# Scan state and its output as whole-array products on a block diagonal, with two state buffers, in a hybrid decoder layer

## The chip, the cores and the metric

The kernel runs on one core of one Trainium2 chip. The metric is the device time in microseconds (us) from launch to end; lower is better. The engines of the core are TensorE (matrix products; PE in the profile, its weight loads PEld), VectorE (DVE), ScalarE (ACT), GpSimd (POOL) and SyncE (SP, which issues DMAs).

## What is computed

One decoder layer over 16 meta tokens and 512 positions, model width 2048, all in fp32: a gated short convolution and an RWKV-7 recurrence side by side on one input projection, an output projection, then a gated feed-forward part. The change touches the recurrence alone. The reference, cut to that:

```python
def rwkv7_scan(r, w, k, v, a_vec, b_vec):
    """All inputs (B, L, H, N) float32. State S (B, H, N_v, N_k):
    S_t = S_{t-1} diag(w_t) + (S_{t-1} a_t) b_t^T + v_t k_t^T ; y_t = S_t r_t."""
    ...
    def step(s, inp):
        r_t, w_t, k_t, v_t, a_t, b_t = inp
        sa = jnp.einsum('bhvk,bhk->bhv', s, a_t)
        s = s * w_t[:, :, None, :] + sa[..., None] * b_t[:, :, None, :] + v_t[..., None] * k_t[:, :, None, :]
        y_t = jnp.einsum('bhvk,bhk->bhv', s, r_t)
        return s, y_t
    s0 = jnp.zeros((bsz, h, n, n), jnp.float32)
    _, ys = lax.scan(step, s0, xs)
    return jnp.swapaxes(ys, 0, 1)
```

There are 16 heads of size 64.

## The kernel before

The sequence of 528 positions is cut into 17 chunks of 32 (`NC`, `C`). Two heads make a pair `P` (128 partitions), two pairs make a scan `s`; so there are 4 scans of 17 chunks, one after the other, each with four heads: `p` is the pair in the scan and `h` the head in the pair. `prep` builds the operands of a pair (among them `XR`, the decayed queries and keys, and `PC`, the decay over a chunk), `inverse` solves the triangular systems within the chunks on VectorE and leaves them in `AT`, and `moves` puts the keys and b vectors into `BK` and the values into `VT`.

`scan(s)` (line 1020) does for each chunk `c`:

- GpSimd copies the chunk's values from `VT` into the state tile `cur` (lines 1029 to 1033). A state tile `SUV` is 128 partitions x 2 pairs x 2 heads x 64: for head `h` the 64 partitions from `64 * h` hold the state, and the other 64 hold the chunk's values and the solved vectors. There are three of them, taken in turn (lines 633 and 1026).
- One product `xp` of `XR` with the whole `cur` (line 1038), four ScalarE copies to `x0`, one product `up` with `AT` (line 1046), and four ScalarE copies of it into `cur`.
- The next state (lines 1059 to 1076): GpSimd multiplies the old state by the decay (`s0`), four products of 64x64 weights from `BK` with 64 columns of `cur` write `sp`, one for each pair and head, and VectorE adds `sp` and `s0` into the next state tile `nxt`.
- The output (lines 1077 to 1083): four products with `cur[:, p, h]` as weights (128 rows, 64 columns) and 32 columns of `XR` write `yp`, and ScalarE copies it to `yt`.

`xp`, `up`, `sp` and `yp` share two PSUM buffers (`st`). All products of the scan are plain fp32. Those of the projections run in the F32R type, on high and low parts of the operands.

The scans run inside the first phase of the kernel, whose other work on TensorE is the input projection (`rkv`, `conv`, written to `mps` and scaled there), LoRA products and block sums. Generators of all tasks are drawn in an order set by a clock of assumed costs (lines 1168 to 1240): the scan's steps have rank 2, the projections' products the rank `FILL`, which stands behind all others. What is drawn is not issued at once: the class `Plan` keeps every instruction with its dependences, and `order` (line 354) makes the order of all engines at once by list scheduling, with the durations of `time` (line 293), the tile shape of a product by `mode` (line 329) and costs for changing it (lines 481 to 484). The engines then run their queues in that order. A product of other than 128x128 weights counts 0.055 there, an fp32 product of the whole array at least 0.222. The scheduler also plans the first and last units of the feed-forward phase; its middle is written in a fixed order.

Since `Engine.__getattr__` issues everything, nearly all rows of the profile name line 231; the tiles tell them apart. In the rows, "st<-SUV,BK" are the state products, "st<-XR,SUV" with 128x64 weights the output products, "st<-SUV,XR" is `xp`, "st<-x,AT" is `up`.

## Time and profile before

| what | us |
|---|---|
| median of 3 runs | 2372.61 |
| the three runs | 2370.54 to 2372.68 |
| profiled execution | 2370.47 |
| its span, from the first to the last instruction | 2368.7 |
| TensorE busy | 2345.2 |
| VectorE busy | 1744.6 |
| ScalarE busy | 1225.2 |
| GpSimd busy | 636.1 |

The profile is of one execution. Its rows give a start or a busy time in us and the mean duration of one instruction in ns. Products are pipelined, so the record of one is longer than the time by which it moves the next; what a product costs is read from the starts of its neighbours. "x8" behind a product counts records, and an fp32 product leaves two (the weights are loaded in two parts).

### The profile page before, as it was taken

The page shows a single profiled execution, that of the slowest core. Times are in us where ns is not written, and L with a number is a line of the kernel's source. Part 1 is how long each engine was busy: PE and PEld are TensorE (multiplying, and loading weights), DVE is VectorE, ACT ScalarE, POOL GpSimd, SP SyncE. Part 2 cuts the span into 40 slices and gives each one's busy share as a digit, 9 for nine tenths or more (in the row PEclk, how much of TensorE's full clock was granted, in tenths as well). Part 3 has the DMA queues.
Part 4 walks back from the last instruction along what each step waited for, and adds up shares of the span by engine and source line. Part 5 has one row for each costly group of instructions (what it writes and reads, how often), then busy time and mean ns, then how long its engine had stood idle before and what let it go on. Part 6 is the DMA issues. An engine that isn't in the chain of part 4 may idle for free.

```text
span 2368.7 us, 46298 instructions
## 1 busy us (share of the span) xinstructions
PE 2345.2 (99%) x18450; PEld 2238.2 (94%) x18450; DVE 1744.6 (74%) x2366; ACT 1225.2 (52%) x2402; POOL 636.1 (27%) x755
## 2 busy tenths in 40 slices
PE   9999999999999999999999999999999999999997
PEld 8999999999999999998989899999999998989897
DVE  7687888878754677784868686777767686859585
ACT  7666766766654555574434343343434342525255
POOL 0232747465351011510202121211212120202025
PEclk9999999999999999999999999999999999999998
DMA  5444332333433755913333323242423242323344
GB/s 185 158 126 122 90 97 83 104 111 98 132 99 95 232 170 178 214 57 100 108 107 103 112 82 124 81 134 81 124 75 125 70 135 79 124 82 105 97 142 90
DMA packets 138759, 274.14 MB, mean 116 GB/s; under 512 B 31120, under 2 KB 54288, under 8 KB 138544
## 3 DMA queue, kind: packets, MB, share of 16 engines
q1 hardware_dynamic: 131760, 264.35, 36.2%
q0 software_dynamic: 6784, 6.83, 2.0%
q8 instruction: 145, 2.38, 0.4%
q14 instruction: 70, 0.57, 0.1%
HBM read 245.30 MB, written 25.84 MB: 114 GB/s over the span
## 4 chain that ended last, share of the span: by engine, by line
PE 96%; DVE 1%; DMA 1%; POOL 1%; ACT 1%; issue 0%; DVEq 0%; SPq 0%; ACTq 0%; POOLq 0%
PE mps L231 60%; PE u L231 18%; PE d L231 11%; PE st L231 4%; PE aux L231 3%; DMA acc<-xT_dram 1%; DVE acc L231 0%; POOL acc L231 0%; PE psn L231 0%; DVE q L231 0%; DMA l<-lo 0%; DMA raw<-w_in_dram 0%; ACT whi L231 0%; POOL XR L231 0%; ACT q L231 0%
## 5 line engine op out<-in xcount | busy, mean ns | idle before, releaser
L231 ACT CAST H<-R 128x1024 fp32r<-128x1024 f32 x401 | 420.4, 1049 | 474.9 <-PE u L231 180.7
L231 DVE TENSOR_TENSOR O<-R,H 128x1024 fp32r<-128x1024 f32 x401 | 521.7, 1301 | 124.2 <-ACT H L231 116.8
L231 PE MATMUL mps<-ahi,whi 128*128 128x264 f32 (+2 forms) x1792 | 360.0, 289 | 6.1 <-ACT ahi L231 5.5
L231 PE MATMUL mps<-alo,whi 128*128 128x264 f32 (+2 forms) x1792 | 360.2, 289 | 0.0
L231 PE MATMUL mps<-ahi,wlo 128*128 128x264 f32 (+2 forms) x1792 | 358.0, 288 | 1.2 <-DVE wlo L231 1.0
L231 PE MATMUL mps<-tt,H 128*128 128x258 f32 x2160 | 288.2, 283 | 1.0 <-ACT q L231 0.9
L231 PEld LDWEIGHTS mps<-ahi,whi 128*128 128x128 f32 x1792 | 273.8, 189 | 9.1 <-ACT ahi L231 5.8
L231 PEld LDWEIGHTS mps<-ahi,wlo 128*128 128x128 f32 x1792 | 274.0, 189 | 3.6 <-DVE wlo L231 1.6
L231 PEld LDWEIGHTS mps<-alo,whi 128*128 128x128 f32 x1792 | 274.0, 189 | 2.8 <-DVE alo L231 0.6
L231 DVE TENSOR_TENSOR wlo<-raw,whi 128x512 fp32r<-128x512 f32 x261 | 199.2, 768 | 104.8 <-ACT whi L231 88.0
L231 PEld LDWEIGHTS mps<-tt,H 128*128 128x128 f32 x2160 | 272.6, 189 | 2.4 <-ACT q L231 1.1
L231 POOL TENSOR_TENSOR raw<-raw,rb 128x516 f32<-128x516 f32 (+1 forms) x45 | 92.8, 2062 | 668.7 <-DVE raw L231 630.6
L231 PE MATMUL mps<-alo,H 128*128 128x258 f32 x1064 | 258.3, 284 | 0.4 <-DVE alo L231 0.4
L231 PE MATMUL mps<-ahi,H 128*128 128x258 f32 x1064 | 258.0, 282 | 0.0
L231 POOL TENSOR_TENSOR R<-R 128x1024 f32<-128x1024 f32 x40 | 131.5, 3287 | 419.1 <-DVE R L231 419.1
L231 ACT CAST whi<-raw 128x512 fp32r<-128x512 f32 x261 | 160.7, 619 | 137.5 <-PE mps L231 83.9
L231 DVE TENSOR_TENSOR R<-R 128x1024 f32<-128x1024 f32 x136 | 226.4, 1665 | 1.7 <-DMA R<-w_pair_dram 0.4
L231 PEld LDWEIGHTS mps<-alo,H 128*128 128x128 f32 x1064 | 198.4, 189 | 0.9 <-DVE alo L231 0.6
L231 PEld LDWEIGHTS mps<-ahi,H 128*128 128x128 f32 x1064 | 198.7, 190 | 0.0
L231 POOL TENSOR_SCALAR SUV<-VT 32x64 f32<-32x64 f32 x272 | 129.4, 476 | 161.4 <-PE st L231 137.5
L231 PE MATMUL mps<-ahi,O 128*128 128x258 f32 x1064 | 157.5, 283 | 0.0
L231 PE MATMUL mps<-tt,O 128*128 128x258 f32 x1080 | 153.4, 281 | 0.0
(339 smaller groups left out, 4593.5 us busy)
## 6 DMA issues: line engine op xcount, KB each, us to landing
R<-w_gu_dram SPq DMA_DIRECT2D x176, 512.0 KB, 3.5
raw<-w_in_dram SPq DMA_DIRECT2D x208, 256.0 KB, 2.7
R<-w_down_dram SPq DMA_DIRECT2D x88, 512.0 KB, 3.7
raw<-w_out_dram SPq DMA_DIRECT2D x32, 256.0 KB, 3.6
R<-w_pair_dram SPq DMA_DIRECT2D x16, 512.0 KB, 4.3
l<-lo SPq DMA_DIRECT2D x24, 264.0 KB, 2.1
R<-ysp SPq DMA_DIRECT2D x14, 257.0 KB, 4.3
lo<-l SPq DMA_DIRECT2D x12, 264.0 KB, 2.6
```

Of the source, the lines that this page charges most:

```text
L231: return getattr(self.real, op)(*real, **{k: x.get() if isinstance(x, View) else x for k, x in kw.items()})
```

## The change

The two heads of a pair are taken together in the state and output products. A new tile `BD` (128 x 2 pairs x 2 heads x 64), set to zero once, gets the chunk's two blocks of `BK` on its diagonal by two GpSimd copies. The state product of a pair then has 128x128 weights (`BD[:, p]`) and 128 columns (both heads of `cur[:, p]`); the blocks of `sp` off the diagonal aren't read. The output product of a pair has `cur[:, p]` of both heads as 128x128 weights and 64 columns of `XR`; of `yp`, too, only the diagonal blocks are read, by two ScalarE copies. There are two state tiles instead of three. In the planner, fp32 products lose their lower bound of 0.222, and a change of type from fp32 to F32R within the whole-array shape counts 0.085.

```diff
@@ -298,9 +298,9 @@
             n *= s
         psum = any(a.tile.pool.space == "psum" for a in x["ins"])
         if e == "PE":
-            if self.mode(x) != (128, 128):
+            if self.mode(x)[:2] != (128, 128):
                 return 0.055
-            return max(0.222, n / 600 + 0.004) if x["args"][1].tile.dtype is F32 else n / 2400 + 0.0115
+            return n / 600 + 0.012 if x["args"][1].tile.dtype is F32 else n / 2400 + 0.0115
         if e == "SP":
             return 0.42
         if e == "POOL":
@@ -329,7 +329,7 @@
     def mode(self, x):
 
         w = x["args"][1]
-        return tuple(next(i for i in (32, 64, 128) if i >= n) for n in (w.parts, int(np.prod(w.shape[1:]))))
+        return tuple(next(i for i in (32, 64, 128) if i >= n) for n in (w.parts, int(np.prod(w.shape[1:])))) + (w.tile.dtype,)
 
     def two(self, x):
 
@@ -440,7 +440,7 @@
         free, busy = dict.fromkeys(HOP, 0.0), dict.fromkeys(HOP, (0.0, False))
         free["PE"] = self.head
         ring = []
-        self.pipe, table, kind = 0.0, 0, (128, 128)
+        self.pipe, table, kind = 0.0, 0, (128, 128, F32R)
         began, ends = [0.0] * len(units), [0.0] * len(units)
         for u in range(len(units)):
             if not left[u]:
@@ -481,7 +481,11 @@
             if e == "PE":
                 k = self.mode(x)
                 if k != kind:
-                    d, kind = d + (0.25 if k == (128, 128) else 0.1), k
+                    if k[:2] != kind[:2]:
+                        d += 0.25 if k[:2] == (128, 128) else 0.1
+                    elif k[2] is F32R:
+                        d += 0.085
+                    kind = k
             began[u], ends[u] = t, start + d
             free[e], busy[e] = start + d, (start + d, self.two(x))
             dma = x["op"] == "dma_start"
@@ -630,10 +634,13 @@
         gmask = cst[:, :64]
         smask = cst[:, 64:]
         SUV = []
-        for i in range(3):
+        for i in range(2):
             t = p1.tile([128, 2, 2, 64], F32, name=f"SUV{i}")
             G.memset(t, 0.0)
             SUV.append(t)
+
+        BD = p1.tile([128, 2, 2, 64], F32, name="BD")
+        G.memset(BD, 0.0)
 
 
         AT = p1.tile([128, NC, 2, 2, C], F32, name="AT")
@@ -1023,7 +1030,7 @@
             f = F3 if s == NP // 2 - 1 else 1
             yt = p1.tile([128, 2, L], F32, name="yt", bufs=2)
             for c in range(NC):
-                cur, nxt = SUV[c % 3], SUV[(c + 1) % 3]
+                cur, nxt = SUV[c % 2], SUV[(c + 1) % 2]
                 b, c0 = (0, 0) if c < CH[1][0] else (1, CH[1][0])
                 BK, VT = st["f", s, b]
                 for h in range(2):
@@ -1057,30 +1064,34 @@
                 elif c > 8:
                     st["late", s] = True
                 if c < NC - 1:
-                    sp = stp.tile([128, 2, 64], F32, name="st")
+                    sp = stp.tile([128, 2, 2, 64], F32, name="st")
+                    for h in range(2):
+                        o = slice(64 - 64 * h, 128 - 64 * h)
+                        G.tensor_scalar(out=BD[o, :, h], in0=BK[o, :, c - c0], scalar1=1.0, scalar2=None, op0=ALU.mult)
+                    for p in range(2):
+                        PE.matmul(sp[:, p], BD[:, p].rearrange("r h k -> r (h k)"), cur[:, p].rearrange("r h v -> r (h v)"),
+                                  start=True, stop=True)
                     for h in range(2):
                         q = slice(64 * h, 64 * h + 64)
-                        o = slice(64 - 64 * h, 128 - 64 * h)
                         if c:
                             if not h:
                                 s0 = p1.tile([128, 2, 64], F32, name="s0")
                             G.tensor_tensor(out=s0[q], in0=cur[q, :, h],
                                             in1=PC[q, :, c - 1].unsqueeze(2).to_broadcast([64, 2, 64]), op=ALU.mult)
-                        for p in range(2):
-                            PE.matmul(sp[q, p], BK[o, p, c - c0], cur[o, p, h], start=True, stop=True)
                     for h in range(2):
                         q = slice(64 * h, 64 * h + 64)
                         if c:
-                            V.tensor_tensor(out=nxt[q, :, h], in0=sp[q], in1=s0[q], op=ALU.add)
+                            V.tensor_tensor(out=nxt[q, :, h], in0=sp[q, :, h], in1=s0[q], op=ALU.add)
                         else:
-                            V.tensor_copy(nxt[q, :, h], sp[q])
-                yp = stp.tile([128, 2, C], F32, name="st")
+                            V.tensor_copy(nxt[q, :, h], sp[q, :, h])
+                yp = stp.tile([128, 2, 2, C], F32, name="st")
                 for p in range(2):
-                    for h in range(2):
-                        q = slice(64 * h, 64 * h + 64)
-                        PE.matmul(yp[q, p], cur[:, p, h], XR[:, c, 1, p, h], start=True, stop=True)
+                    PE.matmul(yp[:, p], cur[:, p].rearrange("r h v -> r (h v)"),
+                              XR[:, c, 1, p].rearrange("r h t -> r (h t)"), start=True, stop=True)
                 n = min(C, L - c * C)
-                S.copy(yt[:, :, c * C:c * C + n], yp[:, :, :n])
+                for h in range(2):
+                    q = slice(64 * h, 64 * h + 64)
+                    S.copy(yt[q, :, c * C:c * C + n], yp[q, :, h, :n])
                 if c == CH[0][1] - 1:
                     st["half", s] = True
                 yield 0.75, D3 * f
```

## Rows read from the trace of the kernel before

**Rows 1.** The page's first part: busy time, share of the span and instructions of each engine; and the span with the mean granted clock of TensorE.

```profile
PE 2345.2 (99%) x18450; PEld 2238.2 (94%) x18450; DVE 1744.6 (74%) x2366; ACT 1225.2 (52%) x2402; POOL 636.1 (27%) x755
...
core 0: 2368.7 us, clock 0.997
```

**Rows 2.** The table of stretches, two of the scan: length, then busy time and instructions of PE, PEld, DVE, ACT and POOL, the granted clock, the DMA share and GB/s.

```profile
300.00:400.00 100.00, 99.57 (x946) 94.56 (x946) 84.25 (x157) 70.39 (x200) 55.61 (x104) 1.00 0.30 87
...
500.00:600.00 100.00, 100.00 (x1009) 95.88 (x1008) 88.33 (x164) 66.26 (x190) 60.47 (x97) 1.00 0.33 100
```

**Rows 3.** Who waited for whom, TensorE alone, over the whole span: total, times, longest.

```profile
PE mps L231 <- ACT ahi L231: 5.5, 1, 5.5
...
PE st L231 <- DVE SUV L231: 0.4, 1, 0.4
```

**Rows 4.** The stretch behind the last scan, from the table of stretches, and the fetches of projection weights between 700 and 900 us, from the view of the tile `raw` (duration in ns, first and last start).

```profile
735.00:760.00 25.00, 25.00 (x211) 25.00 (x211) 15.46 (x25) 10.54 (x18) 3.03 (x2) 1.00 0.36 107
...
L231 SPq DMA_DIRECT2D raw<-w_in_dram x22: 327/328/396, 699.7 to 769.7; - x22
```

**Rows 5.** TensorE's timeline, two stretches: start, length of the merged record, tiles, weight shape, columns, records. First `up` among projection products, then `xp`.

```profile
301.06 0.41 PE L231 MATMUL mps<-ahi,wlo 128*128 128x264 f32 x2
301.31 0.33 PE L231 MATMUL st<-x,AT 128*128 128x64 f32 x2
301.45 0.49 PE L231 MATMUL mps<-ahi,whi 128*128 128x264 f32 x2
301.77 0.41 PE L231 MATMUL mps<-ahi,wlo 128*128 128x264 f32 x2
...
304.89 0.41 PE L231 MATMUL mps<-ahi,wlo 128*128 128x264 f32 x2
305.13 0.60 PE L231 MATMUL st<-SUV,XR 128*128 128x256 f32 x2
...
305.80 0.40 PE L231 MATMUL mps<-alo,whi 128*128 128x264 f32 x2
```

**Rows 6.** The same view around the state and output products of a chunk.

```profile
309.67 0.40 PE L231 MATMUL mps<-ahi,whi 128*128 128x264 f32 x2
310.01 0.45 PE L231 MATMUL st<-SUV,BK 64*64 64x64 f32 x8
310.39 0.42 PE L231 MATMUL st<-XR,SUV 128*64 128x32 f32 x8
...
311.10 0.40 PE L231 MATMUL mps<-ahi,wlo 128*128 128x264 f32 x2
```

**Rows 7.** The same view around 32 transposes (64 records of 64x64), at 149 us alone and at 283 us with a chunk's state and output products behind them: the ordinary pairs before and after.

```profile
149.16 0.41 PE L231 MATMUL mps<-ahi,wlo 128*128 128x264 f32 x2
...
151.86 0.41 PE L231 MATMUL mps<-alo,whi 128*128 128x264 f32 x2
...
283.11 0.40 PE L231 MATMUL mps<-ahi,wlo 128*128 128x258 f32 x2
...
286.44 0.40 PE L231 MATMUL mps<-ahi,whi 128*128 128x258 f32 x2
```

**Rows 8.** The same view around the output products of a scan's last chunk.

```profile
731.61 0.40 PE L231 MATMUL mps<-alo,whi 128*128 128x258 f32 x2
731.94 0.43 PE L231 MATMUL st<-XR,SUV 128*64 128x32 f32 x8
...
732.64 0.40 PE L231 MATMUL mps<-ahi,whi 128*128 128x258 f32 x2
```

**Rows 9.** The same view in the last stage, where every product has a row: the first and the last of 33 products with 320 columns, then the first and the last of 64 with 192 columns.

```profile
2302.37 0.31 PE L231 MATMUL u<-whi,H 128*128 128x320 f32 x1
...
2307.06 0.31 PE L231 MATMUL u<-whi,O 128*128 128x320 f32 x1
...
2337.20 0.28 PE L231 MATMUL u<-whi,ahi 128*128 128x192 f32 x1
...
2344.24 0.28 PE L231 MATMUL u<-hxh,ahi 128*128 128x192 f32 x1
```

**Rows 10.** The view of the tile `st`, weight loads: duration in ns (minimum, median, maximum), first and last start, shapes.

```profile
L231 PEld LDWEIGHTS st<-XR,SUV x544: 132/137/138, 219.9 to 732.1; 128*64 128x64 f32 x182
...
L231 PEld LDWEIGHTS st<-x,AT x136: 186/189/193, 217.4 to 730.0; 128*128 128x128 f32 x136
```

**Rows 11.** Groups of GpSimd's instructions from 220 to 735 us: busy time, mean ns of one, idle time before them and what ended most of it; and GpSimd's longest wait in that stretch, in total.

```profile
L231 POOL TENSOR_SCALAR SUV<-VT 32x64 f32<-32x64 f32 x260 | 125.1, 481 | 153.6 <-PE st L231 137.5
L231 POOL TENSOR_TENSOR s<-SUV,PC 64x128 f32<-64x128 f32 x120 | 64.5, 538 | 17.9 <-DVE SUV L231 10.9
L231 POOL TENSOR_TENSOR XR<-XR,PC 64x1024 f32<-64x1024 f32 x12 | 23.4, 1952 | 10.5 <-PE aux L231 10.0
L231 POOL TENSOR_TENSOR XR<-r,PP 64x544 f32<-64x544 f32 x11 | 15.1, 1374 | 2.4 <-ACT PP L231 1.6
...
POOL SUV L231 <- PE st L231: 137.5, 44, 9.3
```

**Rows 12.** The same view for ScalarE: the copies of the output.

```profile
L231 ACT COPY yt<-st 128x64 f32<-128x64 f32 x64 | 13.6, 212 | 32.5 <-PE st L231 31.4
```

## The prediction

> **What bounds the kernel now.** I read the busy shares first. The matrix engine (TensorE) is busy for 2345.2 of 2368.7 us, at a granted clock of 0.997, so at 2.4 GHz throughout; VectorE and GpSimd are far below [rows 1]. Such an average hides stages, so I next read the table of stretches over the scan, which fills about 150 to 735 us: between 300 and 400 us TensorE idles for 0.4 us, between 500 and 600 not at all, while in the same 100 us GpSimd stands at 56 to 60, ScalarE at 66 to 70 and VectorE at 84 to 88 [rows 2]. The list of what TensorE waited for agrees: the longest is one wait of 5.5 us, and of the scan's products it has only 0.4 us for a state on VectorE [rows 3]. So the scan's chain (product, copies, product, copies, state) is not the limit: between its links TensorE works through the input projection's products, and every product of the scan takes its own time out of a full engine. After the last scan, at 732 us, such filler is still there: TensorE stays full to 760, and projection weights are fetched until 769.7 [rows 4]. **So the change is worth the difference in TensorE's occupancy, plus any new idle time on TensorE.** Latencies elsewhere cost nothing until TensorE waits for them.
>
> **What is removed.** In the timeline of TensorE I take the stretch from the start of the ordinary pair of products ahead of a scan block to the start of the second pair behind it, and subtract two ordinary pairs at 0.245 us (0.25 and 0.24 from start to start [rows 5]). Each fp32 product leaves two records, so x8 is four products. A normal chunk gives 311.10 - 309.67 = 1.43, less 0.49 = 0.94 us for four state and four output products, the way into and out of the small tiles included [rows 6]. In the same view 59 of the 64 chunks that have state products look like this: 55.5 us. Two of the other five stand right behind 64x64 transposes and share their change of tile: 286.44 - 283.11 = 3.33, against 151.86 - 149.16 = 2.70 for transposes alone, so 0.63 us of their own [rows 7]. I price the five at 0.75 each, 3.8 us, since one of them is split and dearer. The four last chunks have output products alone: 732.64 - 731.61 - 0.49 = 0.54 us [rows 8], 2.2 us together. Removed: 61.5 us.
>
> **What is added on TensorE.** A chunk gets two state products (128x128 weights, 128 columns) and two output products (128x128, 64 columns), all fp32. The trace has two relatives. The product of x and AT (128x128, 64 columns) takes 301.77 - 301.06 - 0.49 = 0.22 us, the one with 256 columns 305.80 - 304.89 - 0.49 = 0.42 [rows 5]. A quarter of the columns costs half, so below some width something else sets the price. Two views say that it is the loading of the weights. In the last stage 63 steps of 192-column products take 2344.24 - 2337.20 = 7.04 us, 0.112 each; 32 steps of 320 columns take 4.69 us, 0.147 each, 0.013 over the 0.133 of their columns at 2.4 GHz [rows 9]. By columns 192 would take 0.093, so 0.112 is the floor of one load of 128 weight columns. The 64-column fp32 product is two such loads, 0.224, which is what it measures. And fp32 load records grow from 137 ns for 64 weight columns to 189 for 128 [rows 10]: 52 ns for 64 more, 104 for 128. So the output pair costs 2 x 0.224 = 0.45 us. A state product streams half of 0.42, 0.21, which is below its two loads, so that pair costs 0.45 too. A chunk: 0.90; 64 x 0.90 + 4 x 0.45 = 59.4 us, **2.1 us less than is removed**. Bounds: with the 0.013 of [rows 9] on top of the columns a state record takes 0.12, 1.9 us more in all (gain 0.2); with loads of 104 ns, 528 of them take 54.9 us (gain 6.6). I keep 0.112, since the product that measures it is the output product's own shape.
>
> The Trainium skill (TensorE: Matmul & The Clock Gate, section LDWEIGHTS) lets a weight load take its columns over 1.2, in ns, whatever the rows: 107 ns for 128. The 0.112 step agrees within 5 ns. The rule speaks against this change: whole-array products load twice the columns of half-array ones and gain nothing by their full rows. By 107 ns the sum would be 528 loads, 56.5 us, a gain of 5.0 in place of 2.1.
>
> **Edits off TensorE.** (1) GpSimd fills the block diagonal, two copies a chunk of 64 partitions x 128. No row has that shape. The nearest are the 32x64 copies at 481 ns and the 64x128 two-input products at 538 [rows 11]; I take 0.52, toward the second, which has the size (bounds 0.48 and 0.7). 128 of them are 67 us in some 515 us, of which GpSimd idles about 45%, 137.5 us of it waiting for TensorE at the head of its queue [rows 11]. The price is nothing while each fill ends before its state product. A fill waits for the state product of the chunk before, since there is one block buffer; queued behind it on GpSimd are the copies of V for a later chunk and the decay products, which the state's adds on VectorE want some microseconds later. A chunk takes 7.5 us (68 from 219.9 to 732.1 us [rows 10]), and GpSimd's scan work in it grows from 4 x 0.48 + 2 x 0.54 = 3.0 to 4.0 us. (2) With two state buffers the copies of V into a buffer wait for the output products one chunk before, not two before: still a chunk ahead of need. (3) ScalarE copies the output in two halves, so one copy of 0.21 [rows 12] becomes two of some 0.20: 13 us over the scan on an engine with 30% to spare, and only the reuse of the psum buffer two products later waits for it; uncovered it would delay that by 0.2. (4) VectorE's adds keep their sizes, and the block's memset replaces that of the third state. (5) The cost table feeds the program's own planner, which writes the order of all engines anew: a short fp32 product loses its 0.222 floor there, a return to F32R products costs 0.085. On an engine without idle time another order saves nothing; it can cost. For (1), (2) and (5) together I put 0.5 us of new waits on TensorE, bounds 0 and the price of the second rival.
>
> **Sum.** Against the profiled execution (2370.47 us, of which 2368.7 is span): -2.1 + 0.5 = -1.6, 2368.9. The median of the three runs, 2372.61, lies 2.1 above that execution, so on its scale 2371.0 us.
>
> **Rivals.** *Short fp32 products hide each other's loads.* The start stamps of the x-AT product and of the pair behind it are 0.14 apart [rows 5], 0.07 a record; the other 0.08 of its 0.22 would be paid once, on the return to F32R products, and the new cost table says the same. Then the output pair costs 0.28 + 0.08 and the state pair 0.42 without a return of its own: 0.78 a chunk, 64 x 0.78 + 4 x 0.36 = 51.4, a gain of 10.1 us: 2362.5. Against it: the 192-column step and the load records. The same page of the Trainium skill (section Back-to-back issue gap) gives about 81 ns for a sustained pair of load and product at 128 columns, which would point this way; no row read here has a whole-array step below 0.11.
> *GpSimd is late (slower).* The preparation of a head pair gives GpSimd two products of 64x1024 at 1.95 us and two of 64x544 at 1.37 [rows 11], 6.6 us in bursts. With 4.0 us of scan work in each 7.5, such a burst clears in 6.6/3.5 = 1.9 chunks (1.5 before), and the lead of the V copies falls from two chunks to one. If a fill or those copies stand behind a burst, TensorE stops at the state product or at the next chunk's first product, with all its filler queued behind. At 2 us in each of six preparations that fall into scans this is 12 us, less the 2.1: 2382.5. It decides once a fill ends later than ScalarE's last copy into the state. For it: GpSimd's queue is in order and its waits for TensorE show that it is ordered tightly. Against it: those same 137.5 us of waiting leave room, and TensorE hardly waits today.
> *The tile changes stay.* The 64x64 transposes remain, and where the planner sets them between products they pay their way in and out alone. For the five irregular chunks that is in the sum; elsewhere it is worth some 0.3 us a time, 1 us in all, within the forecast's range.
>
> **How the numbers follow.** The forecast (loads set the price, GpSimd in time) 0.55, its own range 2367 to 2374; hidden loads 0.20; late GpSimd 0.20; anything else 0.05. The range reaches past the first rival and up to the second's price: 2361.5 to 2382. A measurement here tells about 0.2%, 4.7 us, from no change. Faster by more: 0.20 from the first rival and 0.06 from the forecast's lower edge; slower by more: 0.20 from the second and 0.03 of the rest; within: 0.51.
>
> **What would show it.** In the changed trace: a scan block of two state and two output products taking 0.90 us by the same subtraction (0.78 speaks for the first rival), and 64-column output records that add 0.11 each; TensorE idle under 1 us between 300 and 700 us, with no wait for the block or for GpSimd's copies into the state (several us speak for the second rival); GpSimd busy some 13% more of the scan, its wait for TensorE shorter. I am wrong if TensorE idles in the scan, or if the loads of successive fp32 products come closer than 0.11 us.

## The result, and the profile after

| what | before | after |
|---|---|---|
| median, us | 2371.82 (8 runs) | 2379.28 (8 runs) |
| lowest and highest, us | 2370.54 to 2372.68 | 2377.69 to 2380.23 |
| span of the profiled execution, us | 2368.7 | 2378.1 |

The ratio of after to before is 1.0032, with a 95% interval of 1.0022 to 1.0041. The kernel became 7.5 us slower; the forecast was 2371.0, which is no change within what a measurement tells.

The page's first part for the kernel after, as in [rows 1]:

```profile
span 2378.1 us, 45539 instructions
...
PE 2348.1 (99%) x17922; PEld 2255.4 (95%) x17922; DVE 1746.7 (73%) x2366; ACT 1241.5 (52%) x2470; POOL 726.1 (31%) x883
```

TensorE issues 528 product records fewer and its busy time still rises by 2.9 us; busy records of pipelined products overlap, so this tells little. GpSimd's rises by 90 us. Where TensorE stands idle is told by the table of stretches of the kernel after, with the columns of [rows 2]:

```profile
300.00:400.00 100.00, 99.73 (x850) 97.91 (x850) 83.16 (x151) 70.94 (x209) 76.14 (x129) 1.00 0.32 90
...
500.00:600.00 100.00, 97.12 (x872) 94.25 (x873) 81.24 (x149) 67.04 (x197) 76.78 (x119) 1.00 0.33 94
...
220.00:720.00 500.00, 491.65 (x4245) 481.47 (x4245) 394.49 (x698) 348.78 (x1032) 355.02 (x589) 1.00 0.35 99
```

The last row holds most of the scan in both kernels. For the kernel before it is, in the same view:

```profile
0.00:220.00 220.00, 213.57 (x1806) 210.24 (x1808) 163.75 (x288) 147.03 (x278) 40.11 (x82) 1.00 0.49 152
220.00:720.00 500.00, 499.09 (x4825) 475.94 (x4824) 394.63 (x708) 339.81 (x994) 276.55 (x485) 1.00 0.35 101
```

The reader is to see two numbers of the 500 us rows: TensorE's idle time, 500 less its busy time, goes from 0.9 to 8.35 us, and GpSimd's busy time from 277 to 355 us. Ahead of 220 us and behind 720 us the idle time hardly moves (after: 214.00 busy in the first 220 us, against 213.57). So the loss was made in the scan, by idle time on the engine that had none. The granted clock is 1.00 in these rows of both kernels, the 2.4 GHz level.

Who waited for whom, TensorE, of the kernel after (total, times, longest):

```profile
PE mps L231 <- ACT ahi L231: 5.7, 1, 5.7
PE st L231 <- ACT x L231: 4.8, 7, 1.0
PE mps L231 <- DVE wlo L231: 1.3, 2, 1.1
PE st L231 <- POOL SUV L231: 0.9, 2, 0.8
```

The first row is old, the one of 5.5 us in [rows 3]. The two `st` rows concern the scan, and neither names the block `BD`: TensorE stops most at `up`, for ScalarE's copies into `x0` ("x"), and twice for GpSimd's copies into the state.

The scan block itself, TensorE's timeline of the kernel after, as in [rows 6]:

```profile
303.29 0.40 PE L231 MATMUL mps<-ahi,whi 128*128 128x264 f32 x2
303.53 0.61 PE L231 MATMUL st<-SUV,BD 128*128 128x128 f32 x4
303.97 0.56 PE L231 MATMUL st<-XR,SUV 128*128 128x64 f32 x4
304.34 0.49 PE L231 MATMUL mps<-ahi,wlo 128*128 128x264 f32 x2
304.66 0.42 PE L231 MATMUL mps<-alo,whi 128*128 128x264 f32 x2
```

By the forecast's subtraction a chunk's four products take 304.66 - 303.29 - 0.49 = 0.88 us, and the state pair alone 303.97 - 303.53 = 0.44. The same subtraction gives 0.883 on average for 58 of the 64 blocks; with 2.3 for the four last chunks all state and output products come to 58.8 us.

GpSimd's groups of the kernel after from 220 to 745 us, as in [rows 11] (that window ends at 735 us, because the scan ended earlier):

```profile
L231 POOL TENSOR_SCALAR SUV<-VT 32x64 f32<-32x64 f32 x264 | 130.0, 492 | 29.1 <-PE st L231 9.6
L231 POOL TENSOR_SCALAR BD<-BK 64x128 f32<-64x128 f32 x124 | 81.6, 658 | 75.7 <-PE st L231 68.6
L231 POOL TENSOR_TENSOR s<-SUV,PC 64x128 f32<-64x128 f32 x120 | 69.5, 579 | 8.7 <-DVE SUV L231 0.5
```

The fills take 658 ns in the mean, and everything beside them has grown a little (in the mean; 492 against 481, 579 against 538). The waits for TensorE at the head of the queue, 137.5 us at the copies of V before, now stand at the fills, 68.6, and at the copies, 9.6.

One of the stops, from the timeline of the kernel after (GpSimd, ScalarE and the scan's products; in brackets the idle time ahead and its releaser):

```profile
388.55 2.90 POOL L231 TENSOR_TENSOR XR<-r,PP 64x544 f32<-64x544 f32 x2
...
391.54 1.13 POOL L231 TENSOR_SCALAR BD<-BK 64x128 f32<-64x128 f32 x2
...
397.90 2.13 POOL L231 TENSOR_SCALAR BD<-BK 64x128 f32<-64x128 f32 x2
...
401.97 1.77 POOL L231 TENSOR_SCALAR SUV<-VT 32x64 f32<-32x64 f32 x3
...
403.77 1.76 ACT L231 COPY VT<-vt 32x288 f32<-32x288 f32 x4 [1.72 <-POOL SUV L231]
...
405.12 0.59 PE L231 MATMUL st<-SUV,XR 128*128 128x256 f32 x2
...
405.51 1.61 POOL L231 TENSOR_SCALAR BD<-BK 64x128 f32<-64x128 f32 x2
405.54 0.42 ACT L231 COPY yt<-st 64x64 f32<-64x64 f32 x2
...
407.09 0.87 ACT L231 COPY VT<-vt 32x288 f32<-32x288 f32 x2
...
407.97 0.84 ACT L231 COPY x<-st 32x64 f32<-32x64 f32 x4
...
408.87 0.43 PE L231 MATMUL st<-x,AT 128*128 128x64 f32 x2 [1.01 <-ACT x L231]
```

This is read from the bottom up. `up` at 408.87 has waited 1.01 us for the copies into `x0`. Their input, `xp`, was issued at 405.12, but they start only at 407.97, since ScalarE is still working through what its queue holds ahead of them: copies of the output, a cast, and moves of the next values into `VT`. It came to these late: at 402.05 it had to wait 1.72 us at the head of its queue, because `VT` couldn't be overwritten until GpSimd, which runs behind, had copied the chunk's old values out of it (401.97 to 403.74). From 388.55 on GpSimd works with no pause over 0.1 us: two products of the preparation of the next pair, 2.90 us, and behind them two rounds of fills, 1.13 and 2.13 us, among its other work. GpSimd is late, ScalarE stands behind its reads, and TensorE behind ScalarE. No product waits for a fill.

All that ScalarE waited for GpSimd in the scan, first in the kernel after (220 to 745 us), then in the kernel before (220 to 735 us):

```profile
ACT VT L231 <- POOL SUV L231: 5.0, 4, 1.8
...
ACT lo L231 <- POOL zm L231: 3.5, 2, 2.8
...
ACT BK L231 <- POOL BD L231: 2.1, 3, 1.3
```

```profile
ACT VT L231 <- POOL SUV L231: 2.9, 4, 1.9
...
ACT lo L231 <- POOL zm L231: 1.0, 1, 1.0
```

The total goes from 3.9 to 10.6 us. The second row of each is a wait for another product of GpSimd (`zm`); the long one, 2.8 us, ends at 427.06, where that product stood in GpSimd's queue behind a round of fills and three copies of V. The row of `BK` is new in kind: the state products read `BK` before, the fills read it now, so ScalarE's next moves into `BK` stand behind the fills themselves. Of the seven stops at `up` in TensorE's list, six have such a wait of ScalarE in the 6 us ahead of them: at `VT` three (1.26, 1.72 and 1.85 us), at `lo` two (2.81 and 0.71), at `BK` one (1.33). The seventh, of 0.2 us, has none.

Read from the spacing of the products, which also shows stops too short for that list, TensorE stops at 11 chunks at `up` and at 8 at `xp`. Against the usual spacing this costs about 7.5 and 3.2 us; before, 0.25 and 1.4. That is 9 us of stops more, 2.7 us of products less.

### The profile page after: what moved, and what is told of

The parts are those of the page before. It is cut to its first block, busy times and chain, and to the rows that moved or that the text cites. A ratio compares the mean times of both kernels' runs of the same rounds, so it can differ in the third digit from the quotient of the medians.

```text
span 2378.1 us, 45539 instructions
## 1 busy us (share of the span) xinstructions
PE 2348.1 (99%) x17922; PEld 2255.4 (95%) x17922; DVE 1746.7 (73%) x2366; ACT 1241.5 (52%) x2470; POOL 726.1 (31%) x883
## 4 chain that ended last, share of the span: by engine, by line
PE 67%; DVE 1%; DMA 1%; POOL 0%; ACT 0%; issue 0%; DVEq 0%; ACTq 0%; POOLq 0%
PE mps L231 38%; PE u L231 18%; PE d L231 11%; DMA acc<-xT_dram 1%; POOL acc L231 0%; DVE acc L231 0%; DVE q L231 0%; PE st L231 0%; PE psn L231 0%; ACT q L231 0%; DVE tt L231 0%; DVE alo L231 0%; PE aux L231 0%; ACT ahi L231 0%; DVE wlo L231 0%
```

## The experiments

The expectations carry the working names of the theories. The theories with an A lay the loss on GpSimd: on its added time, or (A1) on the planner, whose list of prices has GpSimd's small copies too short, 0.3 us and 0.0011 an element. Those with a B lay it on the state buffers: on the border of two scans (B1), where with two buffers and 17 chunks the last chunk of one scan and the first of the next share a buffer, or on the number of buffers (B2). A third lays it on the planner's new order itself. All runs were timed in five rounds beside the kernel before, whose median was 2371.57, 2371.19, 2371.30 and 2370.72 us in the four groups of four.

All of them together first; the idle time of TensorE and the busy time of GpSimd are those of the row from 220 to 720 us of each:

| run | median, us | ratio to before, 95% | TensorE idle | GpSimd busy | span |
|---|---|---|---|---|---|
| **products of before** | | | | | |
| before | 2371.82 | 1 | 0.91 | 276.6 | 2368.7 |
| e1_two_states | 2375.77 | 1.0020 (1.0011 to 1.0029) | 3.65 | 277.3 | 2374.1 |
| e3_cost_table | 2375.34 | 1.0018 (1.0009 to 1.0026) | 3.60 | 284.1 | 2373.3 |
| e10_before_planner_costs | 2374.33 | 1.0009 (1.0000 to 1.0018) | 4.42 | 282.8 | 2372.5 |
| e14_copies_half_twice | 2384.68 | 1.0057 (1.0045 to 1.0070) | 9.61 | 329.5 | 2384.2 |
| e2_two_states_fills | 2391.24 | 1.0085 (1.0071 to 1.0099) | 14.57 | 347.5 | 2390.2 |
| e15_copies_all_twice | 2408.48 | 1.0155 (1.0141 to 1.0169) | 22.46 | 363.1 | 2406.7 |
| **products of after** | | | | | |
| after | 2379.28 | 1.0032 (1.0022 to 1.0041) | 8.35 | 355.0 | 2378.1 |
| e4_fill_scalar | 2373.35 | 1.0009 (1.0000 to 1.0018) | 3.50 | 274.7 | 2371.7 |
| e7_fill_scalar_alternate | 2373.20 | 1.0008 (0.9999 to 1.0017) | 4.05 | 278.6 | 2371.6 |
| e13_narrow_fills | 2373.18 | 1.0010 (1.0001 to 1.0019) | 4.50 | 325.6 | 2370.9 |
| e8_planner_costs | 2372.15 | 1.0003 (0.9994 to 1.0012) | 3.41 | 357.7 | 2369.5 |
| e12_planner_costs_old_table | 2376.79 | 1.0023 (1.0014 to 1.0033) | 7.59 | 349.2 | 2377.6 |
| e6_three_states | 2381.73 | 1.0044 (1.0030 to 1.0058) | 9.70 | 352.6 | 2379.9 |
| e5_alternate | 2384.76 | 1.0058 (1.0045 to 1.0071) | 10.85 | 349.8 | 2382.7 |
| e11_planner_all | 2388.45 | 1.0077 (1.0065 to 1.0090) | 8.88 | 347.5 | 2386.7 |
| e16_all_costs_narrow_fills | 2389.48 | 1.0078 (1.0065 to 1.0090) | 8.47 | 314.3 | 2387.5 |
| e9_planner_shorter | 2395.46 | 1.0101 (1.0087 to 1.0115) | 15.44 | 335.0 | 2391.2 |

No version beats the kernel before. The ranges set down for the sixteen runs were poor: three medians lie in one (e7 in that of theory C, e8 in that of A1, e15 in that of GpSimd's time), and e9, e13 and e16 miss one by less than 0.5 us. What the runs bear out is directions, and differences between pairs of them.

### One part of the change at a time

**e1_two_states**: before, with two state tiles.

```diff
-        for i in range(3):
+        for i in range(2):
-                cur, nxt = SUV[c % 3], SUV[(c + 1) % 3]
+                cur, nxt = SUV[c % 2], SUV[(c + 1) % 2]
```

> The kernel before with two state buffers in place of three, nothing else. Theory A (the 128 added fills make GpSimd late, and ScalarE's queue and TensorE stop behind it): as before, 2371 to 2373 us, TensorE idle under 1 us from 220 to 735 us. Theory B (two state buffers cost it: the copies of V lose a chunk of lead, and the last chunk of a scan and the first of the next share a buffer): 2378 to 2381, with waits of TensorE where a scan ends. Theory C (the order that the planner writes with the new cost table is worse): as before.

Measured: 1.0020, about 4.7 us. TensorE's list of waits has a new row, which lies at the borders of two scans (by the spacing of products some 4 us there and at the chunk behind):

```profile
PE st L231 <- POOL SUV L231: 1.7, 2, 1.0
```

The last chunk of a scan and the first of the next use the same tile, so GpSimd can bring the new values in only when the old scan's last output product has read the tile. In the timelines the last `xp` of a scan and the first of the next lie 482.44 - 477.41 = 5.0 us apart before, and 490.23 - 482.22 = 8.0 after; TensorE works through other products in that time, and stops for only a part of it. The forecast had left this place out.

**e2_two_states_fills**: e1 and the 128 fills, of a tile that nothing reads, with the old products.

```diff
+        BD = p1.tile([128, 2, 2, 64], F32, name="BD")
+        G.memset(BD, 0.0)
...
+                    for h in range(2):
+                        o = slice(64 - 64 * h, 128 - 64 * h)
+                        G.tensor_scalar(out=BD[o, :, h], in0=BK[o, :, c - c0], scalar1=1.0, scalar2=None, op0=ALU.mult)
```

> The kernel before with two state buffers and with the 128 GpSimd fills of a block-diagonal tile that no product reads; the old products stay. Theory A: 6 to 10 us above the run without the fills, with x0 copies late on ScalarE. Theory B: as the run without the fills, within 1.5 us. Theory C: as the kernel before.

Measured: 1.0085, another 15 us over e1, though no product needs a fill. In this order TensorE stops most at `xp`, for GpSimd's copies into the state themselves, not by way of ScalarE:

```profile
PE st L231 <- POOL SUV L231: 7.8, 5, 2.1
```

The stretch of e2 in which the most is lost:

```profile
220.00:300.00 80.00, 72.77 (x727) 68.54 (x723) 55.34 (x92) 54.50 (x152) 63.61 (x110) 0.96 0.26 78
```

TensorE idles 7.2 of these 80 us, and the granted clock there is 0.96: part of the stretch, in which the engine kept stopping, ran at the lower of the two levels, 1.2 GHz.

**e3_cost_table**: before, with the change's planner table (its hunks of `time`, `mode` and `order` alone).

> The kernel before with the new cost table of the planner alone; the same instructions in another order. Theory A: 2371 to 2373. Theory B: 2371 to 2373. Theory C: 2377 to 2381, with new waits of TensorE in the scan.

Measured: 1.0018. No instruction is added or removed, only the order is another, and it costs 4 us: TensorE's idle time goes from 0.9 to 3.6 us. e1 and e10 have as much; so the order of the kernel before is a good one among its neighbours, and each of these three edits gives it up.

**e4_fill_scalar**: after, with the fills on ScalarE.

```diff
-                        G.tensor_scalar(out=BD[o, :, h], in0=BK[o, :, c - c0], scalar1=1.0, scalar2=None, op0=ALU.mult)
+                        S.copy(BD[o, :, h], BK[o, :, c - c0])
```

> The changed kernel with the block diagonal filled by ScalarE in place of GpSimd (128 copies of some 0.25 to 0.3 us, 35 us on ScalarE). Theory A: GpSimd is as before and the products' gain stays: 2368 to 2372, TensorE's idle time in the scan under 3 us. Theory B: 2378 to 2381. Theory C: 2378 to 2381.

Measured: 1.0009, by the ratios 5.5 us below after, with GpSimd back at 274.7 us and the block still at 0.88 us. Of the loss of after, 5.5 us go when the fills leave GpSimd; but this kernel, too, has an order of its own.

### The buffers

**e5_alternate**: after, with the tile of the first chunk alternating from scan to scan, so that the border shares no tile.

```diff
-                cur, nxt = SUV[c % 2], SUV[(c + 1) % 2]
+                cur, nxt = SUV[(c + s) % 2], SUV[(c + s + 1) % 2]
```

> The changed kernel in which a scan begins with the state buffer that the scan before didn't end with (buffers counted by chunk plus scan). Theory A (the fills make GpSimd late): 2377 to 2380, little change. Theory B1 (two buffers cost at the scans' borders, where last and first chunk share one): 2374 to 2377, and no wait of TensorE for the next scan's first product; the time from the last chunk's first product to the next scan's falls from 8 or 9 us to about 5. Theory B2 (two buffers cost by the lost lead of the V copies): 2378 to 2381.

Measured: 1.0058, slower than after, although the border is mended: its two `xp` lie 497.05 - 492.03 = 5.0 us apart again. What is saved at the borders is lost, and more, at other places; its longest stop, 3.15 us, is at `up` for ScalarE.

**e6_three_states**: after, with three tiles in turn (to make room, the tiles `lr` and `x0` have one buffer instead of two).

> The changed kernel with three state buffers (for the room, one staging tile of the LoRA weights and one x0 tile in place of two). Theory A: 2376 to 2380, the waits behind GpSimd stay. Theory B1: as with alternating buffers. Theory B2: 2370 to 2374.

Measured: 1.0044, not faster than after. With e5 this speaks against the number of buffers as the main cause; but the edit of `x0` touches the very copies that are late, and both kernels have new orders, so it isn't a clean test.

**e7_fill_scalar_alternate**: e4 and e5 together.

> The changed kernel with the fills on ScalarE and the buffers alternating between scans. Theory A with B1: the fills and the border are all that cost, so the products' 2 to 3 us show: 2368 to 2370.5. Theory C (the planner's new order costs by itself): 2372 to 2375.

Measured: 1.0008, the same as e4 alone, and in the range of theory C: without fills on GpSimd and with the border mended the products' gain still doesn't show against before. With GpSimd unburdened, mending the border is worth nothing that can be measured.

### The planner's prices

**e8_planner_costs**: after, with a price of GpSimd's copies in the planner nearer to the profile's rows.

```diff
-                return 0.3 + 0.0011 * n
+                return 0.43 + 0.0014 * n
```

> The changed kernel with one line of the planner's table changed: a GpSimd copy counts 0.43 + 0.0014 per element (0.52 for 32x64, 0.61 for 64x128) in place of 0.3 + 0.0011 (0.37 and 0.44), which is what the trace of the changed kernel shows. Theory A1 (GpSimd has the room, but the order is planned with fills that are too short): 2372 to 2376. Theory A2 (GpSimd's work as such is too much for the stretches in which a pair is prepared): 2377 to 2381. Theory C: anywhere, with other waits.

Measured: 1.0003. The engines do the same work as in after, instruction for instruction (GpSimd 883, ScalarE 2470, TensorE 17922); 7 us come back by the order alone.

**e9_planner_shorter** goes the other way, `0.2 + 0.0008 * n`.

> The changed kernel with the planner's price of a GpSimd copy lowered to 0.2 + 0.0008 per element (0.25 for 32x64, 0.30 for 64x128), further from what the trace shows; the instructions are the same. Theory A1 (the order is planned with fills that are too short): 2382 to 2395, more waits of TensorE behind ScalarE and GpSimd. If every new order merely falls somewhere within a few us: 2371 to 2382.

Measured: 1.0101, 15.44 us of idle time. So far the dose fits: the shorter the planner thinks these copies, the tighter it sets them, and the more TensorE waits.

**e10_before_planner_costs** puts e8's price into the kernel before.

> The kernel before with the truer price of a GpSimd copy (0.43 + 0.0014) in the planner alone. Theory A1, in which the old kernel has so little work on GpSimd that the price hardly matters: 2370 to 2373. If a truer price is worth 7 us to any kernel here: 2364 to 2367.

Measured: 1.0009; the truer price brings nothing where there are no fills.

**e11_planner_all** is e8 with a truer price for GpSimd's decay products too.

```diff
-            return 0.25 + 0.0019 * n if n > 300 else 0.2 + 0.0016 * n
+            return 0.25 + 0.0019 * n if n > 300 else 0.32 + 0.002 * n
```

> The changed kernel with truer prices of GpSimd's copies and of its 64x128 decay products too (0.32 + 0.002 per element, 0.58 for 64x128, in place of 0.405). Theory A1: 2368 to 2372, and TensorE's idle time in the scan under 2 us; the products' own gain of 2 to 3 us would show at 2369.

Measured: 1.0077, against the expectation. Truer prices aren't better in general, so A1 falls in that form. TensorE's list of waits of e11 has, beside one for GpSimd's copies, rows that no GpSimd instruction releases:

```profile
PE st L231 <- POOL SUV L231: 3.5, 3, 2.1
PE aux L231 <- ACT lo L231: 3.2, 2, 2.5
PE st L231 <- DMA AT<-d: 3.2, 1, 3.2
```

**e12_planner_costs_old_table** is after with e8's price and the planner's old table for TensorE.

> The changed kernel with the truer price of a GpSimd copy and the old table of TensorE's costs. Theory A1: 2370 to 2374, as with the new table. Theory C (the new table is worse): 2367 to 2370.

Measured: 1.0023. With e8 this is a pair that differs in the table alone: the new table is worth 0.0020, some 5 us, here, where it cost 4 in e3.

### The same order, another load

Up to here each kernel had an order of its own. In the last four the planner sees the instructions of the kernel that the run starts from, and only what is issued in their places differs.

**e13_narrow_fills**: after's own order; each fill is issued on 8 of the 64 columns of a head and pair. It leaves out most of the block, and so most of the next state's product is not computed; the products keep their sizes.

```diff
+                kw = x["kw"]
+                if isinstance(kw.get("out"), View) and kw["out"].tile.kw.get("name") == "BD":
+                    kw = dict(kw, out=kw["out"][:, :, :8], in0=kw["in0"][:, :, :8])
```

> The changed kernel in its own planned order, with each fill of the block diagonal cut to 8 of 64 columns when it is issued (so the next state misses most of its product); same instructions, engines and dependences, GpSimd some 45 us shorter. If GpSimd's time stops TensorE: 2369 to 2373, with few waits left in the scan. If the order is what costs: 2377 to 2381.

Measured: 1.0010, so 0.0022 below after, some 5 us; in the profiled spans 7.2. GpSimd's group of fills in e13:

```profile
L231 POOL TENSOR_SCALAR BD<-BK 64x16 f32<-64x16 f32 x124 | 46.9, 378 | 93.6 <-PE st L231 87.0
```

That is 81.6 - 46.9 = 34.7 us of GpSimd less. The place of the traced stop, in e13's timeline:

```profile
402.45 1.75 ACT L231 COPY VT<-vt 32x288 f32<-32x288 f32 x4 [0.88 <-POOL SUV L231]
...
404.64 0.59 PE L231 MATMUL st<-SUV,XR 128*128 128x256 f32 x2
...
406.65 0.85 ACT L231 COPY x<-st 32x64 f32<-32x64 f32 x4
...
407.56 0.43 PE L231 MATMUL st<-x,AT 128*128 128x64 f32 x2 [0.42 <-ACT x L231]
```

The same instructions in the same order: ScalarE's wait for GpSimd's reads is 0.88 instead of 1.72, the copies into `x0` start 2.01 us after `xp` instead of 2.85, and `up` waits 0.42 instead of 1.01. The chain is the one traced in after, shortened at its first link alone. ScalarE's waits for GpSimd in all fall from 10.6 to 6.1 us. The median, 2373.18, lies 0.2 above the range for GpSimd's time and far from that for the order.

**e14_copies_half_twice** and **e15_copies_all_twice**: before's own order, with its old products and three states; two, or all four, of a chunk's copies of V are issued twice (136 and 272 instructions more; the last but one line has `< 4` for all four).

```diff
+                o = x["kw"].get("out")
+                if x["op"] == "tensor_scalar" and isinstance(o, View) and str(o.tile.kw.get("name")).startswith("SUV"):
+                    self.extra = getattr(self, "extra", 0) + 1
+                    if self.extra % 4 < 2:
+                        getattr(x["engine"], x["op"])(*x["args"], **x["kw"])
```

> The kernel before in its own planned order, with two of each chunk's four GpSimd copies of V issued twice: 136 more GpSimd instructions, some 65 us, nothing else. If GpSimd's time stops TensorE: 2373 to 2382. If only the order counts: 2370 to 2373.

> The kernel before in its own planned order, with all four GpSimd copies of V of a chunk issued twice: 272 more, some 130 us, close to GpSimd's idle time in the scan. If GpSimd's time stops TensorE: 2385 to 2420, more than twice the loss with half of them. If only the order counts: 2370 to 2374.

Measured: 1.0057 and 1.0155. By the medians of the runs 64 us of added copies cost 14 us (2.7 more than the range for GpSimd's time allows), and 123 us cost 38, in a kernel whose GpSimd stands waiting for TensorE 137.5 us in the scan. TensorE's waits of e14:

```profile
PE st L231 <- ACT x L231: 6.2, 4, 3.7
```

and of e15:

```profile
PE st L231 <- ACT x L231: 13.1, 5, 5.9
PE st L231 <- DVE SUV L231: 6.1, 8, 1.6
```

It is the wait of after again, at `up` for ScalarE, although only GpSimd got more work; in e15 the next state on VectorE, which needs GpSimd's decay product, is late as well. A stretch of e15, where the granted clock falls too:

```profile
400.00:500.00 100.00, 92.82 (x855) 87.72 (x855) 78.07 (x147) 61.57 (x179) 70.70 (x130) 0.97 0.29 87
```

**e16_all_costs_narrow_fills** is e11's order with the narrow fills of e13 (the same part is left out).

> The changed kernel with the truer prices of all GpSimd work (e11) in that same order, with each fill cut to 8 of 64 columns when it is issued (the next state misses most of its product). If GpSimd's time stops TensorE there too: 2370 to 2377, against 2388 with whole fills. If that order is bad by itself: 2385 to 2389.

Measured: 1.0078, the same as e11, with 33 us of GpSimd less. From its list of waits:

```profile
PE st L231 <- DMA AT<-d: 3.7, 1, 3.7
...
PE st L231 <- POOL SUV L231: 2.7, 3, 1.4
```

That order is slow by itself; the fills' time isn't what it pays for.

## Why the prediction was wrong

**What bounds the kernel: right.** TensorE was full, and the time went where it stopped being so. In the table of runs, span and idle time rise together on the whole, from 0.91 and 2368.7 us to 22.46 and 2406.7. e11 and e16 stand out, with spans of some 2387 at less than 9 us: there TensorE also idles 8.75 and 9.05 us ahead of 220 us (6.00 in after) and 5.25 from 720 to 1000 us (2.67 in after), and the granted clock of their row from 220 to 720 us is 0.99 where after has 1.00.

**The products: right, mis-sized by little.** 0.90 us a chunk was forecast, 0.88 measured; 58.8 us added against 61.5 removed, a gain of 2.7 where 2.1 stood. The gain even shows in the totals, if kernels of equal idle time are compared: with 3.4 to 4.5 us of it, e1, e3 and e10 (old products) have spans of 2374.1, 2373.3 and 2372.5, mean 2373.3, and e4, e7, e8 and e13 (new products) 2371.7, 2371.6, 2369.5 and 2370.9, mean 2370.9: 2.4 us less (2.2 by their medians). The rival *Short fp32 products hide each other's loads* falls: it needed 0.78 a chunk. And the state pair, with twice the columns of the output pair, takes the same 0.44, so the columns don't set the price; 0.110 for each of eight loads agrees with the 0.112 step of [rows 9]. The Trainium skill (TensorE: Matmul & The Clock Gate, section LDWEIGHTS) allows 107 ns for 128 weight columns; by it the eight loads of a block would take 0.86, an estimate, and 0.88 was measured. The forecast's remark that this rule speaks against the change was misread: a chunk has half as many products, so its loads have 16 x 64 = 1024 weight columns before and 8 x 128 = 1024 after, and the rule is neutral. What the change gained, 0.94 to 0.88, lies in the way into and out of the small tiles or in the loads of half width; no run separates these.

**The step that failed: "For (1), (2) and (5) together I put 0.5 us of new waits on TensorE".** They measured 7.4 us by the table of stretches, 9 by the spacing of products. The reason given for so little was "The price is nothing while each fill ends before its state product." That condition held: no wait for the block appears on TensorE, and all 64 pairs of fills end before ScalarE's last copy into the state, by 4.4 us in the median. And yet there was a price. Two things stood in place of that step:

- *GpSimd's time costs at other places than at its own product.* A fill delays what is queued behind it, the copies of V; these are late in reading `VT`; ScalarE's next moves into `VT` stand behind that at the head of its queue, as those into `BK` do behind the fills that read it; and the copies into `x0`, which TensorE does need at once, stand behind the moves. Here the runs show the cause and not only the chain: with the order held fixed, less GpSimd time gives back some 5 of after's 7.5 us (e13), and more of it, with nothing else of the change, makes the kernel before slower by 14 and 38 us (e14, e15). Moving the fills to another engine gives back 5.5 (e4), though in another order. The Trainium skill (the same page, section Architectural detail: the array is 16× 32×32, not 1× 128×128) calls ScalarE's and GpSimd's queues strictly first in, first out; the traced stop agrees, with its 1.72 us wait at ScalarE.
- *The order isn't neutral.* "On an engine without idle time another order saves nothing; it can cost" was written, and then priced at next to nothing. e3 changes the order alone and costs 4 us, e8 changes it alone and saves 7. Kernels without added GpSimd work lie between 2371 and 2376 us, those with the fills between 2372 and 2395.

**The rival "GpSimd is late (slower)" was the right mechanism, for the most part with the wrong place.** It forecast 2382.5 with six stops of 2 us, at the state product or the next chunk's first product; there were 19 small ones, 11 of them at `up`, which it didn't name, and 8 at `xp`, which it did (3.2 of 10.7 us; two of them, at borders of scans, for GpSimd itself by the list), and 2379.28. The list has 0.2 us at a state product. That its time is near is in part luck: it had other stops, fewer and longer. Its point of decision, a fill that ends later than ScalarE's last copy into the state, was never met. The argument against it, "those same 137.5 us of waiting leave room", is the misreading behind its 0.20: e14 put 64 us into that room and paid 14. Waiting time at the head of a queue lies where the engine is early. What is added where it is already late, as in the preparation of a pair in the traced stop, can be passed on.

**Sizes of other terms.** A fill: 0.52 us forecast, bounds 0.48 to 0.7; 0.658 in the mean, so 84 us for 128 instead of 67 (GpSimd's busy time in the scan rose by 78, 16% of the stretch instead of 13%). The median of the 128 fills is 0.528; the mean is made by long ones, up to 1.77 us. (2) held within chunks, but the shared tile at the border of scans was overlooked; it stretches each of the three borders by 3 to 4 us, at two of which TensorE stops for GpSimd, 0.9 us in all by its list; when GpSimd is free, e7 shows nothing that can be measured. (3) held in itself, though the stops pass through ScalarE, the engine "with 30% to spare", and (4) held: ScalarE has 9 us more in the 500 us, and TensorE's list has one wait of 0.3 us for a copy of the output, about the 0.2 that was named.

**The account.** 9 us of stops less 2.7 of products is 6.3 of the 9.4 us between the two profiled spans; the last product of `alo` with `whi` into `mps`, at the end of the projections, starts at 878.9 us instead of 870.3, 8.6 later, so nearly all the difference arises ahead of the feed-forward part's middle. Some 2 us between are not accounted for: many small gaps, or records that the trace lacks.

**What stays open.** Which property makes one order better than another: truer prices helped in e8 and hurt in e11. And what share of after's loss each of the two causes has: e13 says 5 us for most of the fills' time in after's order, but e8 gets back 7 with all that time in place and is no slower than e4, which has no fills on GpSimd, so a good order can hide them. What after's own order would cost with no fills at all was not tried.

## What to carry to other kernels

Work moved to an engine with idle time is free only if that time lies where the work is put: look at the places where the engine is last, not at its total of waiting, and follow every reader and writer of the buffers queued behind the new work, since an in-order queue passes lateness on to engines that don't use its result. Ask of the first buffer that another engine must overwrite, not only of the new product. Where a program plans its own order, price any edit with the spread that re-ordering alone gives (here 4 to 7 us), and test a suspected cost with the order held fixed.

## What the runs showed of the hardware that was not expected

- The granted clock fell in stretches in which TensorE idled several us: 0.96 in e2's 220 to 300 us (7.2 us idle in 80) and 0.97 in e15's 400 to 500 us (7.2 in 100), against 1.00 before and after. There the loss exceeds the idle time: e15's span is 38.0 us over that of before, with 21.6 us more idle time in the 500 us. The granted clock of that row of e15 is 0.98 against 1.00, which makes some 10 us of 500 more, an estimate.
- Small GpSimd copies get cheaper by far less than their size: 64x128 elements took 528 ns in the median and 658 in the mean, an eighth of the columns (e13) still 252 and 378.
- The same fill took from 521 to 1771 ns. The Trainium skill (GPSIMD Engine Reference, section 2. Architecture) says that GpSimd's ports to SBUF are shared with VectorE, which is busy 79% of this stretch; no run here separates that from other causes.
